# Low parts of the weights on VectorE instead of GpSimd, outside two attention loops

## The chip, the cores and the metric

The kernel runs on one core of a Trainium2 chip, alone. The metric is the time of one execution on the device in microseconds (us). In the views PE is TensorE (matrix products), DVE VectorE, ACT ScalarE, POOL GpSimd, SP the engine that issues most of the transfers. Every engine works through its own queue of instructions in order.

## What is computed

Two blocks in float32, one after the other, on a sequence of 512 tokens of width 1024, with 256 context tokens in the first. Block one has two layers, each with norm and modulation, attention (first neighborhood, then sliding window), and a squared-ReLU MLP. Block two is an even mixer (differential attention with eight heads, and an mLSTM with four) and an odd mixer (gated spatial mixing).

```python
for i in range(DEPTH):                                   # block one, two layers
    u = modulate(rms_norm(h, g_mix[i]), sh1, sc1)
    h = h + ga1 * (attention_i(u @ wqkv) @ wo)           # neighborhood, sliding window
    h = h + ga2 * squared_relu_mlp(modulate(rms_norm(h, g_mlp[i]), sh2, sc2), w1[i], w2[i])
...
p = rmsnorm(x, pre0) @ l0_w_in                           # even mixer
o_a = rmsnorm(diff_attention(q, k, v, lam)) * silu(z)
hm = rmsnorm(mlstm_chunkwise(q, k, v, i, f) * sigmoid(o)) * silu(z)
x = x + rmsnorm(concat(o_a, hm) @ l0_w_out, post0)
...
y = gelu(u) * (w_spatial * causal @ rmsnorm(gelu(v))) * silu(z)   # odd mixer, from l1_w_in
x = x + rmsnorm(y @ l1_w_out, post1)
```

## The kernel before

Activations are kept transposed: 128 channels on the partitions, tokens in the free dimension, `hl` for the 512 tokens and `hc` for the 256 of the context. A product in float32 is made of three products of parts: each operand is split into a high part, rounded to fp32r, and a low part, the remainder. `split` (L126) does it: ACT copies the source to the high part (L127), and an engine named by the caller subtracts (L128). `load_w` (L133) fetches the weights for 256 columns: two transfers on SP bring raw halves (`wraw`, four buffers), and four splits make `whi` and `wlo` (two buffers each), each a tile of 128x512. The subtractions go to `nc.gpsimd`, unless the caller names another engine. `lin` (L146) and `tok` (L155) multiply: for all chunks of the depth the high weight with both parts of the activation, and last the low weight with the high part (matmuls at L152 and L160). So `wlo` is read in the last third of a product.

The stages, by time in the profile: the first attention loop runs over eight pairs of heads `hp` (54 to 462 us); the first MLP, with the context, 560 to 1098; the sliding window loop over `t`, 1122 to 1322; the second MLP 1396 to 1728; the eight differential heads 1757 to 2030; the four mLSTM heads to 2286; the odd mixer 2365 to 2711. Between them stand `project_back` or `project_out` (products with the output weights, which are added to `hl` or `yacc` by DVE at L418 and L873) and a norm. `rstd` (L259) is the sum of a norm: ACT squares eight tiles, DVE adds them up in `acc` (L268), PE sums over the partitions (L270), ACT makes the root. The next product cannot begin before. The first MLP also carries `ada_vector` (L220), in which DVE multiplies a weight matrix by a vector (`aacc`, L229 and L231).

In a differential head (`attend` L1013) two softmax rows `p` are combined on DVE (L1037 to L1040), transposed on PE (L1043), copied to `pts` on ACT (L1045), and multiplied with the values (`PO`, L1047). Then ACT squares `PO` (L1050), DVE scales it (`t`, L1051), and makes two parts of the square (L1054, L1055) for a sum on PE (`NS`, L1056 and L1057); `gate` multiplies on POOL (L1064) and splits into `yh` and `yl`. In an mLSTM head, `finish` multiplies on POOL (L1218) and DVE (L1227) and splits into `yh` and `yl`; PE makes the states `CU` from `kw` (L1186, L1188).

The order of the instructions on each engine is set by a scheduler when the kernel is built, from the order of the code, from priorities and from estimates of how long each instruction takes. So an instruction that changes its engine moves others too.

Of the kernel before, what the change touches and what calls it, by code (L numbers as in the profile page):

```python
# [62 lines left out]
def kernel(ctx: ExitStack, tc: tile.TileContext, A, out, stop_after=None):  # L63
    nc = tc.nc
# [2 lines left out]
    wp = ctx.enter_context(tc.tile_pool(name="wp", bufs=2))  # L67
    hpool = ctx.enter_context(tc.tile_pool(name="hpool", bufs=1))
    upool = ctx.enter_context(tc.tile_pool(name="upool", bufs=1))
    scr = {}  # L70

    @contextmanager
    def scratch(name, temps, sums):
# [5 lines left out]
    def banks(**tags):  # L79

        turns.clear()
        turns.update((n, itertools.cycle(b)) for n, b in tags.items())

    def bank(n):
        b = next(turns[n])
        return psum.tile([128, 512], F32, name=n, tag=f"b{b}")
# [39 lines left out]
    def split(hi, lo, src, lo_eng):  # L126
        nc.scalar.activation(out=hi, in_=src, func=AF.Copy)  # L127
        lo_eng.tensor_tensor(out=lo, in0=src, in1=hi.bitcast(F32), op=ALU.subtract)  # L128

    def raw_w(kt, n):  # L130
        return wp.tile([128, kt, n], F32, name="wraw", tag="wraw", bufs=4)

    def load_w(parts, kt, n, lo_eng=None, room=None):  # L133
        hi, lo = room or [wp.tile([128, kt, n], F32R, name=x, tag=x) for x in ("whi", "wlo")]
        hk = kt // 2
        for s in (slice(0, hk), slice(hk, kt)):
            raw = raw_w(hk, n)
            for c0, cn, src in parts:
                nc.sync.dma_start(out=raw[:, :, c0:c0 + cn], in_=src.rearrange("(k p) f -> p k f", p=128)[:, s])
            q = hk // 2  # L140
            for x in (slice(0, q), slice(q, hk)):
                y = slice(s.start + x.start, s.start + x.stop)
                split(hi[:, y, :], lo[:, y, :], raw[:, x], lo_eng or nc.gpsimd)
        return hi, lo

    def lin(outs, w, ms, k0=0, k1=KD, start=True, stop=True):  # L146
# [217 lines left out]
    def u_lat():  # L364
        return tuple(upool.tile([128, KD, NLAT], F32R, name=x, tag=x) for x in ("uhl", "ull"))
# [17 lines left out]
    with tc.tile_pool(name="first", bufs=1) as fp, scratch("scr1", 6, 2):  # L383
# [9 lines left out]
        def u_ctx():  # L393
            return tuple(fp.tile([128, KD, NCTX], F32R, name=x, tag=x) for x in ("uhc", "ulc"))
# [133 lines left out]
        def ada_some(it, n):  # L528

            for _ in range(n):  # L530
                next(it, None)

        def neighborhood():
# [4 lines left out]
            with tc.tile_pool(name="na", bufs=1) as ap_:  # L538
# [5 lines left out]
                def qk_proj(hp, w):  # L544
                    qk = []
                    for j in range(2):
                        pl, pc = mm_tile(), mm_tile()[:, :NCTX]
                        lin([(pl, *ul), (pc, *uc)], w, slice(128 * j, 128 * j + 128))
                        g = vec("na_k") if j else nag
                        if j:  # L550
                            y = ky_tile()
                            stack_k(y, LAT, head_norm(pl, NLAT, g))
                            stack_k(y, slice(NLAT, NT), head_norm(pc, NCTX, g))
                            qk.append(y)
                        else:
                            x = qx_tile()
                            lo = next(lows)
                            stack_q((x, lo), LAT, head_norm(pl, NLAT, g))
                            nc.scalar.activation(out=x[:, :, NLAT:QC], in_=x[:, :, 0:64].bitcast(F32), func=AF.Copy)
                            nc.vector.tensor_copy(out=lo[:, :, NLAT:QC], in_=lo[:, :, 0:64].bitcast(F32))  # L560
                            stack_q((x, lo), slice(QC, QC + NCTX), head_norm(pc, NCTX, g))
                            qk.append((x, lo))
                    qks[hp] = qk

                def qk_w(hp, lo_eng=None):
                    return load_w([(0, 128, wqkv[:, 128 * hp:128 * hp + 128]),
                                   (128, 128, wqkv[:, D + 128 * hp:D + 128 * hp + 128])], KD, 256, lo_eng)

                def v_proj(g, ts=range(6)):
                    if g not in wvs:  # L570
                        wvs[g] = load_w([(0, 256, wqkv[:, 2 * D + 256 * g:2 * D + 256 * g + 256])], KD, 256)
                    if g not in vts:
                        vts[g] = vt_tile()
                    vt, wv = vts[g], wvs[g]
                    for t in ts:
                        ps = mm_tile()[:, :256]
                        x, o = (ul, 128 * t) if t < 4 else (uc, 128 * (t - 4))
                        tok(ps, wv, parts(x, slice(o, o + 128)))
                        nc.scalar.activation(out=vt[:, t, :], in_=ps, func=AF.Copy)

                def load_bias(h):
                    nc.sync.dma_start(out=biases[h % 3], in_=A["na_bias"][h])
# [80 lines left out]
                def back(o, k, c, x):  # L663
                    split(o[0][:, k, c], o[1][:, k, c], x, nc.vector)
# [12 lines left out]
                                             start=(j == 0), stop=(j == len(steps) - 1), tile_position=(0, 64 * e))  # L677

                banks(mm="01", AD="2", NS="7", S="34", PT="5", ST="6")
                for hp in range(8):  # L680
                    pv = bank("ST")
                    if hp == 7:
                        oh = (u_lat(), u_ctx())
                    for b in range(5):
                        if b == 1 and hp < 7:
                            qk_proj(hp + 1, qk_w(hp + 1))
                        if b == 1 and hp < 6:
                            v_proj(hp // 2 + 1, range(3, 6) if hp % 2 else range(3))
                        pair = [unit(hp, e, b) for e in range(2)]
                        if b == 4:  # L690
                            pc = bank("ST")
                            attend(hp, b, pair, pc)
                            if hp == 7:
                                back(oh[1], 7, slice(0, NCTX), pc[:, 0:NCTX])
                            else:
                                nc.scalar.activation(out=hc[:, hp, :], in_=pc[:, 0:NCTX], func=AF.Copy)
                        else:
                            attend(hp, b, pair, pv)
                        if b == 3:
                            for c, x in ((slice(64, NLAT), pv[:, 0:NLAT - 64]), (slice(0, 64), pv[:, NLAT - 64:NLAT])):  # L700
                                if hp == 7:
                                    back(oh[0], 7, c, x)
                                else:
                                    nc.scalar.activation(out=hl[:, hp, c], in_=x, func=AF.Copy)
                    for h in range(2 * hp + 3, min(2 * hp + 3 + 2, 16)):
                        load_bias(h)
                    if hp == 7:
                        ws = [load_w([(0, 256, A["na_wo"][:, 256 * x:256 * x + 256])], KD, 256) for x in range(1)]
                    ada_some(ada_rest, (0, 3, 3, 3, 3, 4, 4, 4)[hp])
# [17 lines left out]
        def sliding_window(u):  # L727
# [4 lines left out]
            with tc.tile_pool(name="swa", bufs=1) as ap_:  # L732
# [85 lines left out]
                    return pts, list(range(k0 // 128, k1 // 128)) + [4, 5]  # L818

                banks(mm="0", NS="7", SL="12", SC="3", PT="45", ST="6")  # L820
                for t in range(8):
                    pv = bank("ST")
                    for b in range(4):
                        if b == 1 and t < 7:
                            proj(t + 1)
                        sc = bank("SC")
                        pair = [unit(t, b, e, sc[:, 256 * e:256 * e + 256]) for e in range(2)]
                        order = pair[0][1]
                        for j, c in enumerate(order):
                            for e in (1, 0):  # L830
                                vo = 64 * (2 * (t // 4) + e)
                                nc.tensor.matmul(out=pv[64 * e:64 * e + 64, 128 * b:128 * b + 128], lhsT=vt[:, c, vo:vo + 64],
                                                 rhs=pair[e][0][:, 128 * j:128 * j + 128],
                                                 start=(j == 0), stop=(j == len(order) - 1), tile_position=(0, 64 * e))
                    split(oh[0][:, t, :], oh[1][:, t, :], pv, nc.vector)
                banks(mm="0124", NS="7")
                u = {}
                project_back(1, A["swa_wo"], (oh, None), True, norm_after(1, "mlp", u))
            return u

        stop = {None: 9, "na": 0, "mlp0": 1, "attn1": 2, "mlp1": 3, "even": 4}[stop_after]
        u = neighborhood()
        if stop >= 1:
            nu = {}
# [4 lines left out]
        if stop >= 2:  # L849
            u = sliding_window(u)  # L850
# [613 lines left out]
```

## Time and profile before

| | |
|---|---|
| median of three runs | 2733.99 us (2729.48 to 2734.04) |
| the profiled execution | 2738.25 us, its span 2736.4 us |
| busy: PE, DVE, ACT, POOL | 2603.4 (95%), 1405.6 (51%), 1254.8 (46%), 1087.3 (40%) us |
| low parts `wlo` on POOL (L128) | 628 instructions, 836.4 us |
| mean granted clock of PE | 0.99 of full speed |

The busy shares are means over stages with different limits. What a change is worth in a stage is read from the waits of the engine that sets the pace there. A wait is put down to the instruction that came last before it ended. In the timeline, instructions of one engine that follow each other at once may be shown as one row with a count.

### The profile page before, as it was taken

Reading aid. Unit: us, or ns where it says so; the run is one execution under the profiler, and the core shown is the slowest. Engines: PE = TensorE matmul, PEld = TensorE weight load, DVE = VectorE, ACT = ScalarE, POOL = GpSimd, SP = SyncE. Lnnn points to the kernel's source line nnn. Section 1 sums busy time; section 2 is a strip of 40 time slices with the busy share of each in tenths; the row PEclk is TensorE's granted clock in tenths of the full one; section 3 lists DMA queues with packets and bytes.
Section 4 is the critical chain, followed back from the end, with each engine's and each line's share of the span. In section 5 each row is a group of like instructions: output and inputs, shape, how many; then the busy total and the mean of one; then the engine's idle time right before and its main releaser. Section 6 shows DMA issues by size and latency. Waiting matters only on the chain. (4 is left out here: it accounts for less than half of the span.)

```text
span 2736.4 us, 40968 instructions
## 1 busy us (share of the span) xinstructions
PE 2603.4 (95%) x15876; PEld 2201.9 (80%) x15876; DVE 1405.6 (51%) x2908; ACT 1254.8 (46%) x2664; POOL 1087.3 (40%) x932
## 2 busy tenths in 40 slices
PE   6999998999999999899999999899999999899998
PEld 4877776788888889777888888877778888898887
DVE  4667667675666567688552222544553444502024
ACT  5655555422222223588543332466654554544342
POOL 3221313333332322533254544544435555435453
PEclk9999999999999999999999999999999999999999
DMA  7211324243333342210123333322222222322321
GB/s 246 61 55 56 107 63 153 66 135 100 114 117 118 92 124 62 74 32 19 45 88 97 93 100 100 81 62 62 67 66 78 78 83 72 97 80 91 95 87 62
DMA packets 217635, 237.94 MB, mean 87 GB/s; under 512 B 9824, under 2 KB 179296, under 8 KB 217440
## 3 DMA queue, kind: packets, MB, share of 16 engines
q1 hardware_dynamic: 210464, 229.15, 27.7%
q10 hardware_dynamic: 6976, 6.17, 0.7%
q8 instruction: 125, 2.05, 0.3%
q14 instruction: 70, 0.57, 0.1%
HBM read 233.18 MB, written 2.10 MB: 86 GB/s over the span
## 5 line engine op out<-in xcount | busy, mean ns | idle before, releaser
L128 POOL TENSOR_TENSOR wlo<-wraw,whi 128x512 fp32r<-128x512 f32 x628 | 836.4, 1361 | 887.3 <-ACT whi L127 847.3
L152 PE MATMUL mm<-uhl,whi 128*128 128x512 f32 (+1 forms) x1480 | 574.3, 391 | 3.6 <-ACT whi L127 2.6
L152 PE MATMUL mm<-ull,whi 128*128 128x512 f32 (+1 forms) x1480 | 569.9, 388 | 4.3 <-POOL ull L128 2.1
L127 ACT ACTIVATE whi<-wraw 128x512 fp32r<-128x512 f32 (+1 forms) x632 | 354.0, 619 | 445.2 <-issue 276.7
L152 PE MATMUL mm<-uhl,wlo 128*128 128x512 f32 (+1 forms) x1480 | 406.3, 386 | 0.0
L152 PEld LDWEIGHTS mm<-uhl,whi 128*128 128x128 f32 x1480 | 282.0, 191 | 62.8 <-ACT whi L127 6.1
L152 PEld LDWEIGHTS mm<-ull,whi 128*128 128x128 f32 x1480 | 282.2, 191 | 56.9 <-POOL ull L128 3.7
L152 PEld LDWEIGHTS mm<-uhl,wlo 128*128 128x128 f32 x1480 | 270.2, 190 | 54.1 <-issue 2.2
L418 DVE SCALAR_TENSOR_TENSOR hl<-mm,mod,hl 128x512 f32<-128x512 f32 (+1 forms) x156 | 105.2, 679 | 226.9 <-PE mm L152 226.9
L152 PE MATMUL mm<-h1h,whi 128*128 128x512 f32 (+1 forms) x576 | 208.4, 369 | 0.0
L152 PE MATMUL mm<-h1l,whi 128*128 128x512 f32 (+1 forms) x576 | 208.1, 369 | 0.0
L152 PE MATMUL mm<-h1h,wlo 128*128 128x512 f32 (+1 forms) x576 | 161.8, 368 | 0.0
L160 PE MATMUL mm<-whi,uhl 128*128 128x256 f32 x608 | 155.0, 290 | 1.0 <-DVE t L297 0.5
L160 PE MATMUL mm<-whi,ull 128*128 128x256 f32 x608 | 152.9, 287 | 0.0
L231 DVE SCALAR_TENSOR_TENSOR aacc<-araw,csil,aacc 128x512 f32<-128x512 f32 x196 | 148.5, 811 | 2.5 <-DMA araw<-ada_w 2.4
L304 POOL TENSOR_TENSOR t<-t,t 128x512 f32<-128x512 f32 (+1 forms) x46 | 49.1, 1067 | 231.5 <-ACT t L301 132.1
L479 DVE TENSOR_TENSOR t<-mm,t 128x512 f32<-128x512 f32 (+1 forms) x96 | 53.1, 574 | 153.2 <-ACT t L474 153.1
L474 ACT ACTIVATE t<-mm 128x512 f32<-128x512 f32 (+1 forms) x100 | 47.7, 507 | 177.8 <-PE mm L152 177.8
L152 PE MATMUL mm<-ulc,whi 128*128 128x256 f32 x448 | 124.6, 286 | 1.1 <-POOL ulc L128 1.1
L152 PE MATMUL mm<-uhc,whi 128*128 128x256 f32 x448 | 124.8, 287 | 0.0
L152 PEld LDWEIGHTS mm<-h1h,whi 128*128 128x128 f32 x576 | 108.6, 188 | 19.6 <-issue 1.0
L152 PEld LDWEIGHTS mm<-h1l,whi 128*128 128x128 f32 x576 | 108.6, 189 | 18.7
(381 smaller groups left out, 5445.2 us busy)
## 6 DMA issues: line engine op xcount, KB each, us to landing
wraw<-mlp_w SPq DMA_DIRECT2D x128, 512.0 KB, 3.8
wraw<-l_w_in SPq DMA_DIRECT2D x88, 512.0 KB, 3.7
araw<-ada_w SPq DMA_DIRECT2D x112, 256.0 KB, 3.0
wraw<-l_w_out SPq DMA_DIRECT2D x32, 512.0 KB, 3.5
wraw<-ada_w SPq DMA_DIRECT2D x24, 512.0 KB, 4.2
wraw<-l_w_in SPq DMA_DIRECT2D x48, 256.0 KB, 3.3
wraw<-na_wqkv SPq DMA_DIRECT2D x32, 256.0 KB, 3.8
wraw<-swa_wqkv SPq DMA_DIRECT2D x12, 512.0 KB, 3.6
```

The lines of the kernel that those rows point to most:

```text
L127: nc.scalar.activation(out=hi, in_=src, func=AF.Copy)
L128: lo_eng.tensor_tensor(out=lo, in0=src, in1=hi.bitcast(F32), op=ALU.subtract)
L152: nc.tensor.matmul(out=o[0], lhsT=a[:, i, ms], rhs=o[j][:, i, :], start=(start and n_ == 0), stop=(stop and n_ == len(terms) - 1))
L160: nc.tensor.matmul(out=ps, lhsT=x[:, i, :], rhs=w[:, i, :], start=(n_ == 0), stop=(n_ == len(terms) - 1))
L231: nc.vector.scalar_tensor_tensor(out=acc[v], in0=raw, scalar=x, in1=acc[v], op0=ALU.mult, op1=ALU.add)
L304: nc.gpsimd.tensor_tensor(out=q, in0=q, in1=r, op=ALU.mult)
L418: nc.vector.scalar_tensor_tensor(out=o, in0=ps, scalar=mod[i][:, 8 * which + m, v:v + 1], in1=h, op0=ALU.mult, op1=ALU.add)
L474: nc.scalar.activation(out=a, in_=p, func=AF.Relu)
L479: nc.vector.tensor_tensor(out=q, in0=p, in1=a, op=ALU.mult)
```

## The change

`scr["lo"]` holds the engine that makes the low parts in `load_w`. It is VectorE from the start; GpSimd from before the first attention loop until its last pass (`hp == 7`), and again around the sliding window loop.

```diff
-    scr = {}
+
+    scr = {"lo": nc.vector}
...
-                split(hi[:, y, :], lo[:, y, :], raw[:, x], lo_eng or nc.gpsimd)
+                split(hi[:, y, :], lo[:, y, :], raw[:, x], lo_eng or scr["lo"])
...
                 banks(mm="01", AD="2", NS="7", S="34", PT="5", ST="6")
+                scr["lo"] = nc.gpsimd
                 for hp in range(8):
                     pv = bank("ST")
                     if hp == 7:
+                        scr["lo"] = nc.vector
                         oh = (u_lat(), u_ctx())
...
                 banks(mm="0", NS="7", SL="12", SC="3", PT="45", ST="6")
+                scr["lo"] = nc.gpsimd
                 for t in range(8):
...
                     split(oh[0][:, t, :], oh[1][:, t, :], pv, nc.vector)
+                scr["lo"] = nc.vector
```

The instructions of the program are the same 588 subtractions on another engine, but the scheduler then orders all the queues anew. Three places, in the order of the queue (line numbers of the changed kernel are 1 to 5 higher).

DVE in the norm before the first MLP, before (`acc` is the sum of the squares `t`, `aacc` the running sum of `ada_vector`):

```order
783 L268 TENSOR_TENSOR acc<-acc,t_5444 128x256
784 L231 SCALAR_TENSOR_TENSOR aacc<-araw,csil,aacc 128x512
785 L268 TENSOR_TENSOR acc<-acc,t_5447 128x256
786 L231 SCALAR_TENSOR_TENSOR aacc<-araw,csil,aacc 128x512
787 L268 TENSOR_TENSOR acc<-acc,t_5450 128x256
788 L231 SCALAR_TENSOR_TENSOR aacc<-araw,csil,aacc 128x512 x3
789 L280 SCALAR_TENSOR_TENSOR t_5457<-hc,gmlp_94,rstd 128x256
```

and now:

```order
796 L269 TENSOR_TENSOR acc<-acc,t_5444 128x256
797 L232 SCALAR_TENSOR_TENSOR aacc<-araw,csil,aacc 128x512
798 L269 TENSOR_TENSOR acc<-acc,t_5447 128x256
799 L232 SCALAR_TENSOR_TENSOR aacc<-araw,csil,aacc 128x512
800 L269 TENSOR_TENSOR acc<-acc,t_5450 128x256
801 L232 SCALAR_TENSOR_TENSOR aacc<-araw,csil,aacc 128x512 x2
802 L129 TENSOR_TENSOR wlo<-wraw,whi 128x512
803 L281 SCALAR_TENSOR_TENSOR t_5457<-hc,gmlp_94,rstd 128x256
```

The rows up to the last `acc` are the same; the first `wlo` of the next weights stands behind it.

DVE in the norm at the start of the even mixer, before (`hl` is the residual stream being updated by the last product of the MLP):

```order
1862 L268 TENSOR_TENSOR acc<-acc,t_16788 128x256
1863 L268 TENSOR_TENSOR acc<-acc,t_16791 128x256
1864 L418 SCALAR_TENSOR_TENSOR hl<-mm,mod_91,hl 128x256
1865 L268 TENSOR_TENSOR acc<-acc,t_16794 128x256
1866 L268 TENSOR_TENSOR acc<-acc,t_16797 128x256
1867 L418 SCALAR_TENSOR_TENSOR hl<-mm,mod_91,hl 128x256
1868 L268 TENSOR_TENSOR acc<-acc,t_16800 128x256
1869 L268 TENSOR_TENSOR acc<-acc,t_16803 128x256
1870 L268 TENSOR_TENSOR acc<-acc,t_16806 128x256
```

and now:

```order
2013 L269 TENSOR_TENSOR acc<-acc,t_16788 128x256
2014 L129 TENSOR_TENSOR wlo<-wraw,whi 128x512
2015 L419 SCALAR_TENSOR_TENSOR hl<-mm,mod_91,hl 128x256
2016 L269 TENSOR_TENSOR acc<-acc,t_16791 128x256
2017 L129 TENSOR_TENSOR wlo<-wraw,whi 128x512
2018 L419 SCALAR_TENSOR_TENSOR hl<-mm,mod_91,hl 128x256
2019 L269 TENSOR_TENSOR acc<-acc,t_16794 128x256
2020 L129 TENSOR_TENSOR wlo<-wraw,whi 128x512
2021 L269 TENSOR_TENSOR acc<-acc,t_16797 128x256
2022 L129 TENSOR_TENSOR wlo<-wraw,whi 128x512
2023 L269 TENSOR_TENSOR acc<-acc,t_16800 128x256
2024 L129 TENSOR_TENSOR wlo<-wraw,whi 128x512
```

Between nearly every two sums a `wlo` now stands, five in front of the last one.

ACT at the end of the third differential head, before (`pts` are copies of the transposed rows, `sz` a gate, `t_17949` the square of the head's output):

```order
1302 L1045 ACTIVATE pts<-PT 128x384
1303 L997 ACT_TABLE_LOAD
1304 L997 ACTIVATE sz<-mm 128x512
1305 L1045 ACTIVATE pts<-PT 128x512
1306 L1050 ACTIVATE t_17949<-PO 128x512
1307 L127 ACTIVATE whi<-wraw 128x512 x2
```

and now:

```order
1299 L1050 ACTIVATE pts<-PT 128x384
1300 L1038 ACT_TABLE_LOAD
1301 L1038 ACTIVATE p,l_17930<-p,nm 128x512
1302 L128 ACTIVATE whi<-wraw 128x512 x4
1303 L1050 ACTIVATE pts<-PT 128x512
1304 L1002 ACT_TABLE_LOAD
1305 L1002 ACTIVATE sz<-mm 128x512
1306 L1055 ACTIVATE t_17949<-PO 128x512
```

The four `whi` of the next weights, two of which stood behind the square, now stand in front of the last `pts`.

## Rows read from the trace of the kernel before

**Rows 1.** MLP one, MLP two, odd mixer: start:end length, PE PEld DVE ACT POOL, PEclk, DMA

```profile
560.00:1098.00 538.00, 535.18 (x3306) 466.15 (x3305) 335.60 (x525) 141.28 (x290) 167.80 (x124) 1.00 0.35 106
1396.00:1728.00 332.00, 331.52 (x1567) 278.86 (x1566) 98.04 (x141) 106.27 (x197) 157.69 (x120) 1.00 0.31 96
2365.00:2711.00 346.00, 346.00 (x1941) 302.74 (x1940) 63.54 (x113) 150.43 (x302) 168.77 (x132) 1.00 0.27 83
```

**Rows 2.** waits of PE: line, what ended them; us in total, times, longest us

```profile
PE NS L270 <- DVE acc L268: 38.3, 10, 16.5
PE PT L1043 <- DVE p L1040: 8.6, 8, 2.0
PE NS L270 <- DVE pr L1007: 7.1, 1, 7.1
PE NS L1057 <- DVE t L1055: 5.1, 7, 0.7
PE CU L1188 <- DVE kw L1186: 4.9, 3, 1.7
PE mm L152 <- DVE yl L128: 2.2, 1, 2.2
```

**Rows 3.** groups by shape, wlo on POOL and on DVE: count | busy, mean ns | idle

```profile
L128 POOL TENSOR_TENSOR wlo<-wraw,whi 128x512 fp32r<-128x512 f32 x624 | 833.6, 1365 | 884.3 <-ACT whi L127 847.3 <-PE mm L152 17.3 <-issue 10.9
L128 DVE TENSOR_TENSOR wlo<-wraw,whi 128x512 fp32r<-128x512 f32 x4 | 2.6, 687 | 0.1
```

**Rows 4.** timeline, DVE and POOL, norm before the first MLP: start us, us, engine, line

```profile
526.95 1.51 DVE L268 TENSOR_TENSOR acc<-acc,t 128x256 f32<-128x256 f32 x1
528.38 1.77 DVE L231 SCALAR_TENSOR_TENSOR aacc<-araw,csil,aacc 128x512 f32<-128x512 f32 x1
533.15 0.41 DVE L268 TENSOR_TENSOR acc<-acc,t 128x256 f32<-128x256 f32 x1
533.48 0.74 DVE L231 SCALAR_TENSOR_TENSOR aacc<-araw,csil,aacc 128x512 f32<-128x512 f32 x1
526.43 6.25 POOL L128 TENSOR_TENSOR wlo<-wraw,whi 128x512 fp32r<-128x512 f32 x4 [1.41 <-ACT whi L127]
```

**Rows 5.** timeline, DVE, norm at the start of the even mixer

```profile
1735.85 2.93 DVE L268 TENSOR_TENSOR acc<-acc,t 128x256 f32<-128x256 f32 x2
1740.36 4.90 DVE L268 TENSOR_TENSOR acc<-acc,t 128x256 f32<-128x256 f32 x3
```

**Rows 6.** timeline, DVE, last head of the first attention loop

```profile
446.11 0.48 DVE L651 TENSOR_SCALAR p<-p,rl 128x512 f32<-128x512 f32 x1
447.68 1.52 DVE L651 TENSOR_SCALAR p<-p,rl 128x512 f32<-128x512 f32 x1
```

**Rows 7.** timeline, DVE and PE, norms before the second MLP and behind the even mixer

```profile
1374.68 4.32 DVE L268 TENSOR_TENSOR acc<-acc,t 128x256 f32<-128x256 f32 x5
1381.86 0.70 PE L270 MATMUL NS<-acc,ones 128*128 128x256 f32 x2 [4.23 <-DVE acc L268]
2322.08 0.96 DVE L268 TENSOR_TENSOR acc<-acc,t 128x256 f32<-128x256 f32 x1
2327.34 2.55 DVE L268 TENSOR_TENSOR acc<-acc,t 128x256 f32<-128x256 f32 x2
```

**Rows 8.** timeline, DVE and POOL, one differential head

```profile
1883.15 1.43 DVE L1039 TENSOR_SCALAR p<-p,l 128x256 f32<-128x256 f32 x1
1887.52 0.40 DVE L1039 TENSOR_SCALAR p<-p,l 128x384 f32<-128x384 f32 x1
1895.59 1.40 POOL L1064 TENSOR_TENSOR t<-t,sz 128x512 f32<-128x512 f32 x1 [11.16 <-DVE t L1051]
```

**Rows 9.** timeline, DVE, one mLSTM head

```profile
2142.89 3.35 DVE L1227 SCALAR_TENSOR_TENSOR nctionType.Sigmoid<-nctionType.Sigmoid,vecs,t 128x512 f32<-128x512 f32 x2 [0.27 <-ACT t L1225]
```

**Rows 10.** the same view as rows 1, behind the norm before the first MLP

```profile
532.70:539.50 6.80, 4.89 (x12) 3.84 (x13) 6.45 (x14) 2.98 (x7) 0.39 (x1) 0.50 0.61 194
```

**Rows 11.** timeline, ACT, another differential head

```profile
1864.30 1.15 ACT L127 ACTIVATE whi<-wraw 128x512 fp32r<-128x512 f32 x2 [1.53 <-PE mm L152]
```

## The prediction

> **What bounds the kernel now.** The stretches come first. TensorE (PE) is the bound: in the first MLP, the second MLP and the odd mixer it is busy for 535.18 of 538 us, 331.52 of 332 and 346.00 of 346 [rows 1]. Nothing that happens on VectorE (DVE) or GpSimd (POOL) can shorten those 1216 us by more than 3.3. What can be won is the time in which PE stands still, so the next view is the table of PE's waits [rows 2]. It names DVE in nearly every row that matters: the sum for the norms (acc, L268) 38.3 us in ten waits, of which one of 16.5 us lies before the first matmul and is not touched, so 21.8 remain; 7.1 us at the start of the even mixer (the name there is pr, but it stands behind the acc's, and these are late); the softmax row p in the differential heads (8.6), t L1055 there (5.1), the state kw in the mLSTM heads (4.9), yl once (2.2).
>
> Then why DVE is late there. A low part wlo takes 1365 ns on POOL and 687 ns on DVE for the same 128x512 tile [rows 3]. More important is what a running wlo does to DVE. In the norm before the first MLP an acc takes 0.41 us when POOL rests and 1.51 us beside POOL's four wlo, an aacc 0.74 and 1.77 us [rows 4]. At the start of the even mixer three acc's take 4.90 us [rows 5], where three short ones would take 1.2. In this kernel the two engines hold each other up, about 1 us a meeting.
>
> **The change, part by part.** By the order of the instructions 588 subtractions go from POOL to DVE, and 52 stay on POOL inside the two attention loops. On DVE they are 588 x 0.687 = 404 us of work. Instructions on DVE start a little before the one in front has ended: the short acc's and aacc's at 533.15, 533.48 and so on come 0.33 us apart at 0.41 us long [rows 4], so I count 0.61 us of the queue for a wlo and 0.33 for an acc. In the full stretches I cost them at nothing: in the first MLP DVE is busy for 335.60 of 538 us, a good part of that held up by POOL, in the second 98.04 of 332, in the odd mixer 63.54 of 346 [rows 1]. The cover is DVE's idle time; without it each would cost 0.61 us.
>
> Now place by place, in PE's time.
>
> A, the norm before the first MLP. Two acc's and two aacc's are each about 1.05 us too long (1.51 less 0.41, 1.77 less 0.74; one of each stands) [rows 4]. In the new order no wlo stands in front of the last acc of this norm: 4 x 1.05 = 4.2, all inside the wait with which PE starts the sum. Bounds 3 to 5.
>
> B, the last head of the first attention loop, whose loads now go to DVE too. p L651 takes 1.52 us beside POOL's wlo where another of the same shape takes 0.48 [rows 6]; nine operations of that head are too long in this way, by 7 us in all. Eleven subtractions of 0.61 us come into the same queue. I take 3; bounds 0 (they fall on the same rows) and 7 (they fall between).
>
> C, the norm before the second MLP and the one behind the even mixer's last project_out. In the first, five acc's take 4.32 us instead of about 2.0, and PE starts 7.2 us after they began, behind a wait of 4.23 [rows 7]. In the new order six acc's, one L418 (0.40) and four wlo stand there: 2.0 + 0.4 + 2.4 = 4.8, and PE follows 0.1 later: gain 2.3. In the second, from the first slow acc (0.96) to the end of the last two (2.55) it is 7.8 us [rows 7]; seven acc's, three L873 and three wlo make 2.3 + 1.0 + 1.8 = 5.1: gain 2.7, of which I take 2.4 for a slower start. Together 4.7; bounds 0 (a wlo waits for its whi in front of an acc) and 9 (no wlo is in the way).
>
> D, the norm at the start of the even mixer. From the first slow acc at 1735.85 to the end of the last at 1745.26 it is 9.4 us [rows 5]. In the new order seven acc's, two L418, five wlo, pr and one ql stand there: 2.3 + 0.8 + 3.1 + 0.1 + 0.4 = 6.7. Gain 2.7; bounds 0 and 5.4 (all the excess).
>
> E, the differential heads. In every second head POOL's four wlo meet the first softmax rows: L1039 takes 1.43 us where a larger one, unhindered, takes 0.40 [rows 8]. PE's waits for p are 8.6 us in eight, on average 1.1 [rows 2]. Three heads give 1.1 less 0.3 for the wlo that now stand between these rows, 2.4 in all; the last head, where wlo and rows alternate, 2.0. Together 4.4; bounds 0 and 8.6. The 5.1 us for t L1055 I leave as they are: what holds it up is POOL's gate product L1064, which runs there for 1.40 us [rows 8] and stays on POOL.
>
> F, the mLSTM heads. The two L1227 take 3.35 us [rows 9]; the first would take 0.61, the second still meets POOL's yl and takes 1.55: 1.2 gained in each of three heads, out of the 4.9 us for kw. In the last head POOL has three wlo queued in front of a product that yl needs, and the 2.2 us for yl go [rows 2]. Together 5.8; bounds 2 and 7.
>
> G, the clock. After a long wait PE runs for a while at the lower of its two levels, 1.2 GHz: a granted clock of 0.50 for 6.8 us after the wait of A, with 4.89 us of matmuls in it [rows 10], which would take half at 2.4 GHz: 2.45. A stretch after yl's wait costs 1.7. These two I count as gone, 4.2; the others stay, since most of a wait stays in front of them. Bounds 0 and 10.
>
> H, new waits. In heads 0, 2 and 4 of the differential attention ScalarE (ACT) now has four whi in front of the last pts, and whi waits until PE has released the weight buffer. Two such whi take 1.15 us behind a wait of 1.53 [rows 11], so four are 2.3 and pts follows 0.6 later: 2.9. Between the release and the product that reads pts PE has eleven matmuls of 128x512, at 331.52/1567 = 0.21 us [rows 1] 2.3 us. That leaves 0.6, with the hand-overs about 1 in each of three heads: 3; bounds 0 and 7 (the whole 2.3 three times).
>
> The sum is 4.2 + 3 + 4.7 + 2.7 + 4.4 + 5.8 + 4.2 - 3 = 26.0 us. The profiled execution took 2738.25 us, 4.3 above the median of the runs shown, 2733.99. So 2738.25 - 26.0 - 4.3 gives 2708.0: **2708**. Late next at A, C and D is DVE still, then ACT's squares.
>
> **Rivals.** *The meetings stay.* Some 290 operations remain on POOL outside the loops (ull, yl, gates, t L304), and each of the 588 is now one that they can meet. If half of what A to F win comes back in this form, 24.8 become 12.4, the clock gives 1 and H costs 3: 10.4, or 2723.6. For it speaks that t L1055 meets POOL's gate in all eight heads [rows 8]; against it that POOL's work falls by 588 x 1.365 = 800 us. The Trainium skill, page "SBUF — State Buffer", section "Who interferes with whom", says that a VectorE instruction with two SBUF inputs contends with a GpSimd instruction that reads SBUF, and that whoever issues first keeps the other out for the whole instruction. The rows agree (1.51 us against 0.41); and by this rule a moved subtraction, with its two inputs, is itself such an instruction.
>
> *The exchange is even.* At C, D and E the wlo stand in front of the last acc or between the rows, and take from the same chain what the meetings took. If they arrive late or take 0.9 us of the queue, C and D keep 4 of 7.4, B and E nothing, the clock nothing, A and F their 10, and H costs 10: 4 in all, 2730.
>
> *Slower: DVE stands behind its own wlo.* Of POOL's idle time 847.3 us were waits of a wlo for its whi [rows 3]; that cost nothing, since hardly anything else was queued there. On DVE the evictions L418 and L479, the acc's and the softmax rows are queued behind each wlo. PE runs on while free PSUM banks last, up to seven of twelve or more matmuls, 7 x 12 x 0.21 = 18 us; a wait of DVE that is longer stops it. If one in two of the 143 moved loads stopped PE for 1 us, 72 less 26 leave 46 us: 2780. Against it: in the new order nearly every wlo stands behind the work that is due before it.
>
> **Chances.** Forecast 0.73, the meetings stay 0.11, the even exchange 0.09, slower 0.07. The range runs from 2690, where B to H go 18 of the 25 us to their better bounds, to 2729, which takes in the second case and half of the third. A measurement of this kernel can tell about 0.2%, 5.5 us, from no change. Faster by more: the first case and most of the second, 0.82; within it 0.11; slower 0.07.
>
> **What would show it.** DVE's work up by 404 us less what the meetings took (1 us each), POOL's down by 800; acc at 0.41 us in the norm before the first MLP, and PE's wait there near 1 us; PE's waits for acc, without the first, near 13 us; L1039 below 0.5 us in the heads; two fewer stretches at 1.2 GHz; the full stretches within 1 us of what they were. It is wrong if PE waits for evictions or for wlo inside the MLPs, if acc keeps its two lengths in the norms, or if ACT's whi in front of pts stop PE for more than 2 us a head.

## The result and the profile after

The changed kernel takes 2671.83 us (median of five runs, 2669.24 to 2673.70) where the kernel before takes 2732.59; the ratio is 0.9779 with an interval of 0.9765 to 0.9793. That is 60.8 us faster, where 26.0 were forecast, with a range that ended at 2690. The direction and the mechanism on VectorE were right, the size was not: what the new order does to PE's own queue was left out, and most of the clock with it.

The profiled execution has a span of 2667.5 us, 68.9 less than that of before. PE's busy time fell by 21.8 us, from 2603.4, and its idle time by 47.1. Some 8 of the 68.9 us are which executions were profiled: that of before took 5.7 us more than its median, that of now 2.6 less. The shares of the engines, then what is left of PE's waits (as in [rows 2]), then the full stretches (as in [rows 1]):

```profile
PE 2581.6 (97%) x15876; PEld 2185.8 (82%) x15876; DVE 1611.9 (60%) x3496; ACT 1249.7 (47%) x2661; POOL 314.9 (12%) x344
```

```profile
PE NS L271 <- DVE acc L269: 22.3, 10, 14.8
...
PE NS L1062 <- DVE t L1060: 5.1, 7, 0.7
...
PE mm L153 <- POOL ull L129: 2.9, 5, 1.0
...
PE mm L153 <- DVE wlo L129: 1.9, 3, 0.8
```

```profile
541.10:1076.40 535.30, 534.81 (x3306) 466.27 (x3305) 361.77 (x652) 142.40 (x293) 6.39 (x8) 1.00 0.35 109
1364.80:1696.40 331.60, 331.60 (x1567) 278.94 (x1566) 163.27 (x263) 107.46 (x200) 0.00 (x0) 1.00 0.31 96
...
2296.10:2642.10 346.00, 346.00 (x1941) 302.74 (x1940) 121.57 (x225) 150.48 (x302) 25.60 (x20) 1.00 0.27 83
```

The waits for acc, without the first one, are 7.5 us instead of 21.8, and those for pr, p, kw and yl are gone. DVE's busy time rose by 206 us although 404 us of work came to it. Of the difference, some 150 us are meetings that no longer happen: added up one by one in the trace, the lengths of DVE's other instructions fell from 1542 to 1391 us. The rest is mostly that instructions which follow each other at once overlap by 0.08 us, so a subtraction adds less than its length. The groups by shape show the same (line, form, count, busy us, mean ns; acc before and after):

```profile
L129 DVE TENSOR_TENSOR wlo<-wraw,whi 128x512 fp32r<-128x512 f32 x576 | 384.2, 706 | 380.8 <-ACT whi L128 248.3 <-PE mm L153 81.0 <-PE mm L161 50.4
...
L268 DVE TENSOR_TENSOR acc<-acc,t 128x256 f32<-128x256 f32 x101 | 64.5, 638 | 22.6 <-ACT t L266 19.3
...
L269 DVE TENSOR_TENSOR acc<-acc,t 128x256 f32<-128x256 f32 x101 | 43.6, 432 | 13.6 <-ACT t L267 11.4
...
L1232 DVE SCALAR_TENSOR_TENSOR nctionType.Sigmoid<-nctionType.Sigmoid,vecs,t 128x512 f32<-128x512 f32 x8 | 5.6, 747 | 0.0
```

Where the time went, stage by stage, from the two profiled executions. A stage ends in both where PE has issued the same number of matmuls; the clock's column is the length of the stretches at 1.2 GHz.

| stage (us in the trace of before) | length before, after | PE idle before, after | at 1.2 GHz before, after |
|---|---|---|---|
| the start (to 54) | 54.3, 51.7 | 22.1, 19.0 | 0, 0 |
| first loop, without its last head (54 to 410) | 355.8, 352.7 | 17.7, 16.3 | 3.4, 0 |
| its last head (to 462) | 52.1, 47.6 | 7.4, 5.5 | 3.4, 0 |
| norms before the first MLP (526 to 560) | 34.1, 25.1 | 8.4, 2.6 | 10.2, 0 |
| first MLP (to 1098) | 537.8, 535.3 | 2.8, 0.5 | 0, 0 |
| norms before the sliding window (to 1122) | 24.0, 18.1 | 5.7, 1.6 | 3.4, 0 |
| norm before the second MLP, with its product (1322 to 1396) | 74.0, 69.4 | 5.9, 2.7 | 3.4, 0 |
| start of the even mixer (1728 to 1757) | 29.0, 20.7 | 7.3, 1.2 | 10.2, 0 |
| differential heads (to 2030) | 273.1, 260.0 | 19.3, 10.6 | 3.4, 0 |
| mLSTM heads (to 2286) | 256.0, 251.3 | 5.0, 0.7 | 0, 0 |
| behind the even mixer (to 2365) | 78.9, 67.7 | 10.5, 4.6 | 13.7, 0 |

The other stages differ by less than 1.1 us. In this execution not one of the eleven stretches at 1.2 GHz inside the program is left, only the one at its end. The four other executions of the changed kernel have a mean granted clock of 0.996 or 0.997; one stretch of 3.4 us takes 0.0006 off the mean, so by this estimate they have one to four such stretches inside. The mean granted clock (the line of the core, before and after):

```profile
core 0: 2736.4 us, clock 0.989
```

```profile
core 0: 2667.5 us, clock 0.998
```

And the norm at the start of the even mixer, which had the longest wait inside the program [rows 2, 5], in the timeline (PE before; then DVE and PE after):

```profile
1745.31 1.22 PE L270 MATMUL NS<-acc,ones 128*128 128x256 f32 x2 [7.09 <-DVE pr L1007]
```

```profile
1707.37 0.41 DVE L269 TENSOR_TENSOR acc<-acc,t 128x256 f32<-128x256 f32 x1
1707.70 0.68 DVE L129 TENSOR_TENSOR wlo<-wraw,whi 128x512 fp32r<-128x512 f32 x1
1708.31 0.41 DVE L269 TENSOR_TENSOR acc<-acc,t 128x256 f32<-128x256 f32 x1
...
1707.50 0.50 PE L153 MATMUL mm<-uhl,wlo 128*128 128x256 f32 x2 [0.83 <-DVE wlo L129]
...
1710.90 0.70 PE L271 MATMUL NS<-acc,ones 128*128 128x256 f32 x2 [0.17 <-DVE acc L269]
```

The sums take 0.41 us each and the wlo between them 0.68, as the prediction counted. But PE, which had stood still for 7.09 us in front of this sum, is now nearly always busy with products that use the new wlo; it waits 0.83 us for one of these and 0.17 us for the sum. In front of this sum PE has 41 matmuls of the next product in its queue; before it had 16. The scheduler filled up in the same way at three more norms: 26 instead of 16 before the second MLP, 32 instead of 19 at the context norm, and 12 more behind the even mixer. In the norm before the first MLP nothing changed there.

### The profile page after: what moved, and what is told of

The parts are those of the page before. It is cut to its first block, busy times and chain, and to the rows that moved or that the text cites. A ratio compares the mean times of both kernels' runs of the same rounds, so it can differ in the third digit from the quotient of the medians.

```text
span 2667.5 us, 40938 instructions
## 1 busy us (share of the span) xinstructions
PE 2581.6 (97%) x15876; PEld 2185.8 (82%) x15876; DVE 1611.9 (60%) x3496; ACT 1249.7 (47%) x2661; POOL 314.9 (12%) x344
## 4 chain that ended last, share of the span: by engine, by line
PE 80%; DVE 10%; ACT 7%; issue 2%; DMA 1%; POOL 0%; DVEq 0%; POOLq 0%; ACTq 0%; SPq 0%
PE mm L153 59%; PE mm L161 7%; PE ST L677 1%; DVE t L281 1%; PE PT L656 1%; PE ST L836 1%; PE PT L819 1%; PE NS L300 1%; DVE acc L269 1%; PE S L347 1%; PE PO L1052 1%; ACT qx L327 1%; DVE wlo L129 1%; ACT whi L128 1%; ACT qx L333 1%
## 5 line engine op out<-in xcount | busy, mean ns | idle before, releaser
L129 DVE TENSOR_TENSOR wlo<-wraw,whi 128x512 fp32r<-128x512 f32 (+1 forms) x580 | 385.7, 704 | 383.6 <-ACT whi L128 248.3
L129 POOL TENSOR_TENSOR ull<-t,uhl 128x256 fp32r<-128x256 f32 (+1 forms) x40 | 37.7, 947 | 1091.5 <-ACT uhl L128 997.8
L232 DVE SCALAR_TENSOR_TENSOR aacc<-araw,csil,aacc 128x512 f32<-128x512 f32 x196 | 135.2, 746 | 0.0
L161 PEld LDWEIGHTS mm<-whi,uhl 128*128 128x128 f32 x608 | 116.2, 191 | 2.7 <-DVE t L298 1.4
## 6 DMA issues: line engine op xcount, KB each, us to landing
araw<-ada_w SPq DMA_DIRECT2D x112, 256.0 KB, 2.9
wraw<-l_w_in SPq DMA_DIRECT2D x48, 256.0 KB, 3.4
wraw<-na_wqkv SPq DMA_DIRECT2D x32, 256.0 KB, 4.0
```

Of the source, the lines that this page charges most:

```text
L161: nc.tensor.matmul(out=ps, lhsT=x[:, i, :], rhs=w[:, i, :], start=(n_ == 0), stop=(n_ == len(terms) - 1))
L232: nc.vector.scalar_tensor_tensor(out=acc[v], in0=raw, scalar=x, in1=acc[v], op0=ALU.mult, op1=ALU.add)
```

## Theories

*Meetings:* the gain is that DVE and POOL no longer hold each other up; whether it is the wlo that runs on POOL does not matter, only that POOL reads SBUF. *Readiness:* the gain is that a wlo is done sooner, and that the scheduler therefore puts more of the next product in front of the sums. *The clock* amplifies either. The experiments are the changed kernel with one thing put back or moved on, unless something else is said.

## Experiments

**e1 and e2: work on GpSimd that nobody reads.** The order of the other engines is left as it is.

```diff
+        if n == 256:
+            nc.gpsimd.tensor_copy(out=dmy[:, 0:1], in_=hs(2)[:, 0:1])
+            for _ in range(4):                                                # e1
+                nc.gpsimd.tensor_tensor(out=dmy, in0=dmy, in1=dmy, op=ALU.mult)
+            for _ in range(10):                                               # e2
+                nc.gpsimd.memset(dmy, 0.0)
```

> The changed kernel (2671.8 us) plus work on GpSimd that nobody reads: in each norm over 256 columns, once the third tile of its input is there, one copy of a column and four products 128x512 of two SBUF operands (about 5.5 us a norm). The order on TensorE, VectorE and ScalarE is the same as in the changed kernel, instruction by instruction. If the gain came from the meetings of VectorE and GpSimd, acc takes 1 us or more again in these norms, TensorE's waits for acc come back at eight or nine norms with 2 to 4 us each, and so do stretches at 1.2 GHz: 2692 to 2707 us. If it came from wlo being ready sooner, or from the new order alone: 2671 to 2676 us.

> As e1, with ten memsets of 128x512 in place of the four products, about as long in all (5.5 us a norm) and at the same places; again the order on the other engines is that of the changed kernel. If a GpSimd instruction holds VectorE up because it reads SBUF, a memset does not: acc stays at 0.41 to 0.47 us, 2671 to 2677 us. If any busy GpSimd does it, or what counts is the ull and other work queued behind on GpSimd, the time is that of e1: 2692 to 2707 us.

e1 takes 2695.21 us, 23.4 more than the changed kernel, e2 2673.33, 1.5 more. The same wlo, the same place in DVE's queue, beside products (e1; DVE, POOL) and beside memsets (e2; DVE, POOL):

```profile
1716.08 1.52 DVE L131 TENSOR_TENSOR wlo<-wraw,whi 128x512 fp32r<-128x512 f32 x1
...
1715.95 3.72 POOL L270 TENSOR_TENSOR dmy<-dmy 128x512 f32<-128x512 f32 x3
```

```profile
1705.00 0.68 DVE L131 TENSOR_TENSOR wlo<-wraw,whi 128x512 fp32r<-128x512 f32 x1
...
1706.00 0.41 DVE L275 TENSOR_TENSOR acc<-acc,t 128x256 f32<-128x256 f32 x1
...
1704.53 1.70 POOL L270 MEMSET dmy<- 128x512 f32 x3
```

PE's waits for acc, in e1 and in e2:

```profile
PE NS L277 <- DVE acc L275: 36.9, 11, 17.9
```

```profile
PE NS L277 <- DVE acc L275: 23.5, 9, 14.8
```

Beside products this wlo takes 1.52 us, beside memsets 0.68, and the next acc there 0.41. So what holds DVE up is not that POOL is busy, nor what is queued there, but what it does. The Trainium skill, page "SBUF — State Buffer", section "Who interferes with whom", says that a VectorE instruction with two SBUF inputs contends with a GpSimd instruction that reads SBUF, not with one that only writes it; the two runs agree. e1 also shows the prediction's first rival at work on the moved subtractions themselves. Of the 25.5 us between the profiled executions of e1 and of the changed kernel, 10.6 lie behind the even mixer, where PE's idle time rose by 7.7.

**e3, e9 and e12: the filling in front of the sums.** PE's matmuls beyond a given number are queued behind the sum, as they were before. e3 does it at the start of the even mixer, e9 and e12 at four norms. A few instructions on DVE and ACT change places with them: at the start of the even mixer six wlo instead of five stand in front of the last acc.

```diff
-                nc.tensor.matmul(out=o[0], lhsT=a[:, i, ms], rhs=o[j][:, i, :], ...)
+                with tc.issue_after(hold.ins) if hold and n_ >= free else nullcontext():
+                    nc.tensor.matmul(out=o[0], lhsT=a[:, i, ms], rhs=o[j][:, i, :], ...)
...
-                qk_proj(0, w0, HALF[x:x + 1])
-                v_proj(0, range(2 * x, 2 * x + 2))
+                qk_proj(0, w0, HALF[x:x + 1], None if x else half_sum)
+                with nullcontext() if x else tc.issue_after(half_sum.ins):
+                    v_proj(0, range(2 * x, 2 * x + 2))
```

> The changed kernel with one thing put back as it was before, at the start of the even mixer alone: on TensorE only the first 16 matmuls of the next projection may stand in front of the norm's sum, the 25 others of it stand behind (as in the kernel before). If the gain at this norm (8.3 us) is largely the longer filling in front of the sum, TensorE waits there 3 to 4 us again (25 x 0.12), with a stretch at 1.2 GHz behind it: 3 to 7 us slower, 2675 to 2679. If the gain is that of the shorter chain on VectorE alone: no change, 2671 to 2673.

> As e3, but at four norms: the start of the even mixer, the norm before the second MLP, the context norm before the sliding window and the norm behind the even mixer's last project_out. In front of each sum TensorE has again as many matmuls of the next product as in the kernel before (16, 16, 19 and 12, where the changed kernel has 41, 26, 32 and 24). If the longer filling is what the prediction missed, e3's 5.8 us grow by 1 to 2 us of waiting at each of the three others, with a stretch at 1.2 GHz behind some: 2680 to 2690 us. If it counts at the even mixer alone: 2677 to 2679.

> e9 mended at its fourth place. There e9 held back three products too many behind the sum; now exactly the twelve matmuls stand behind it that stood behind it in the kernel before, and the four norms have the filling of before. The three other places gave back 9 us in e9. If the filling is what the prediction missed there too: 12 matmuls, 1.4 us of waiting and a longer one at 1.2 GHz, 2 to 5 us on top of the nine: 2682 to 2686 us. If the filling does not count at the fourth place: 2680 to 2682.

e3 takes 2677.61 us, 5.8 more; e9 2688.17, 16.3 more; e12 2682.12, 10.3 more. In e9 the fourth place held three products too many back, and PE waited 10.3 us there, nearly twice as long as in the kernel before; so of e9 only the other three places count, and e12 is the one to read. At the context norm e12 (like e9) still goes too far: 15 matmuls stand in front of the sum where the kernel before has 19, which at 0.12 us each is about 0.5 us of its wait there. In e12, PE's waits for acc, the wait at the start of the even mixer, and the clock around its end:

```profile
PE NS L272 <- DVE acc L270: 32.8, 9, 15.0
```

```profile
1716.18 1.22 PE L272 MATMUL NS<-acc,ones 128*128 128x256 f32 x2 [5.36 <-DVE acc L270]
```

```profile
1713.30:1720.20 6.90, 4.02 (x15) 3.60 (x16) 4.60 (x11) 1.54 (x5) 0.00 (x0) 0.51 0.86 227
```

The wait of 7.09 us falls to 5.36 with the filling of before, so by the faster DVE, and from there to 0.17 by the filling. At the three other norms (before the second MLP, context, behind the even mixer) the waits were 4.23, 2.73 and 5.36 us before, are 2.71, 2.35 and 3.40 in e12, and 0.53, 0.32 and 1.98 in the changed kernel:

```profile
1353.07 0.70 PE L271 MATMUL NS<-acc,ones 128*128 128x256 f32 x2 [0.53 <-DVE acc L269]
...
2266.61 0.67 PE L271 MATMUL NS<-acc,ones 128*128 128x256 f32 x2 [1.98 <-DVE acc L269]
```

So at these four norms more than half of what PE won is the order of its own queue, which is worth about 10 of the 60.8 us, the clock included. Why the scheduler filled up so was not taken apart.

**e4: the gate product on VectorE.**

```diff
-                nc.gpsimd.tensor_tensor(out=t, in0=t, in1=szs[h // 2][h % 2], op=ALU.mult)
+                nc.vector.tensor_tensor(out=t, in0=t, in1=szs[h // 2][h % 2], op=ALU.mult)
```

> The changed kernel with the gate product of the eight differential heads (t times sz) on VectorE instead of GpSimd. If it is GpSimd's product that holds up the low part of the square, that operation takes 0.69 instead of 1.66 us, TensorE's seven waits for it (5.1 us in the changed kernel too) fall below 1 us in all: 3 to 5 us faster, 2667 to 2669. If the product stands in the same chain on VectorE instead: within 1 us of 2671.8.

2665.58 us, 6.3 less, a little more than the 3 to 5 expected. The low part of the square (line 1060 in this kernel too; min, median, max in ns) took 1658 ns in the changed kernel (the median), and now:

```profile
L1060 DVE TENSOR_TENSOR t<-t,t x8: 679/683/685, 1763.9 to 1966.3; 128x512 fp32r<-128x512 f32 x8
```

PE's idle time in the stage fell by 4.0 us. What the prediction said of this wait, that POOL's gate product makes it and keeps it, was right.

**e5 and e13: the differential heads.** Low parts of the loads back on GpSimd, in e5 inside the loop over the heads, in e13 up to the end of the product behind it.

```diff
             banks(mm="012", NS="7", S="34", PT="5", PO="6")
+            scr["lo"] = nc.gpsimd
             for h in range(8):
...
+            scr["lo"] = nc.vector            # e5
             gate_rows(ps)
             project_out(A["l0_w_out"][0:D, :], (yh, yl), yacc, True)
+            scr["lo"] = nc.vector            # e13
```

> The changed kernel with the low parts of the loads inside the loop over the eight differential heads back on GpSimd. This stage is 13.1 us shorter in the changed kernel than before. If it is the low parts of this stage that did it, the 13 us come back: 2682 to 2686 us, with TensorE's waits for the softmax rows at 8 us again. By the prediction's own terms for this stage (4.4 us, with one stretch at 1.2 GHz 6): 2676 to 2678.

> e5, with the loads of the product behind the differential heads (project_out) on GpSimd as well. e5 gave back 7.8 us of the 13.1 of this stage. If the rest is the last head, where the low parts of these loads meet the softmax rows: the stage is back at 271 to 273 us, 2683 to 2686 us in all. If it is the new order of the stage that no low part on GpSimd brings back: 2679 to 2681.

e5 takes 2678.87 us, 7.0 more, which lies between its two expected ranges, with 7.8 of the stage's 13.1 back; e13 2683.29, 11.5 more, with 12.6 back. PE's waits for the softmax rows in e5 and e13:

```profile
PE PT L1048 <- DVE p L1045: 5.7, 6, 1.5
```

```profile
PE PT L1048 <- DVE p L1045: 8.6, 8, 2.0
```

8.6 us is what they were before [rows 2]. So nearly all of this stage is the low parts, and some 5 us of it those of the output weights, which meet the last head's rows. Both runs put back the meetings together with POOL's slower subtraction and the order that goes with it; how much each is worth was not taken apart.

**e6: the full stretches.**

```diff
-                        w = load_w([(0, 256, w1[...])], KD, 256)
+                        w = load_w([(0, 256, w1[...])], KD, 256, nc.gpsimd if g > 1 else None)
...
-                        ws.append(load_w([(0, 512, w2[...])], 4, 512))
+                        ws.append(load_w([(0, 512, w2[...])], 4, 512, nc.gpsimd if g < 6 else None))
...
-                w = load_w([(0, 256, wi[...])], KD, 256)
+                w = load_w([(0, 256, wi[...])], KD, 256, nc.gpsimd)
```

> The changed kernel with the low parts back on GpSimd inside the stretches that TensorE fills: the loads of both MLPs but for their first and last ones, and the input loads of the odd mixer, some 270 of the 588 moved subtractions. If nothing on VectorE or GpSimd counts while TensorE is full: 2670 to 2674 us, with VectorE held up about 1 us a meeting again and nobody waiting. If the change also paid there: 3 to 8 us slower.

2674.43 us, 2.6 more, a little above the expected range. In the profiled executions the three stretches are as long as in the changed kernel (535.0, 331.6 and 346.1 us), and most of the difference lies in four single stretches at 1.2 GHz in stages that the edit does not touch; such stretches of 3.4 us (1.7 us of time each) come and go from run to run. So 256 of the 588 moved subtractions are worth 2.6 us at most, and in the three stretches themselves nothing, as forecast.

**e7, e8, e10 and e11: further on.** e7 has no low part of a weight on GpSimd at all; e8 has the changed kernel's loads, with ull, ulc, the odd halves of the residual sum, and the gate and yl of the differential heads on VectorE; e10 is both; e11 moves the rest of the arithmetic as well.

```diff
-                scr["lo"] = nc.gpsimd                                   # e7, e10, e11: at both loops
+                scr["lo"] = nc.vector
...
-                split(uh, ul, t, nc.gpsimd)                             # e8, e10, e11
+                split(uh, ul, t, nc.vector)
...
-            (nc.gpsimd if k % 2 else nc.vector).tensor_tensor(out=hl[:, k, c], ...)
+            nc.vector.tensor_tensor(out=hl[:, k, c], ...)
...
-        nc.gpsimd.tensor_tensor(out=q, in0=q, in1=r, op=ALU.mult)       # e11, and others like it
+        nc.vector.tensor_tensor(out=q, in0=q, in1=r, op=ALU.mult)
```

> The changed kernel with VectorE also inside the two attention loops of the first block, so that no low part of a weight is made on GpSimd at all (52 more subtractions, 36 us of work on VectorE). In these loops VectorE is busy for 280 of 408 us and 156 of 200. If the meetings cost more than the subtractions even there: 2 to 6 us faster, 2666 to 2670. If VectorE sets the pace in the loops: 2 to 10 us slower, 2674 to 2682.

> The changed kernel with nearly all that still meets VectorE in norms and heads moved off GpSimd: the low parts ull and ulc of the modulated input, yl and the gate of the differential heads, and the odd halves of the residual sum behind the mixers. If meetings are what is left to win, TensorE's waits for ull and ulc (4.7 us) and for the square (5.1) go: 5 to 10 us faster, 2662 to 2667. If these operations now stand in VectorE's chain in front of what TensorE waits for: no gain or up to 6 us slower, 2672 to 2678.

> e7 and e8 in one: no low part of a weight on GpSimd anywhere, and the work of norms and differential heads on VectorE. The two gains (10.3 and 26.9 us) lie in different stages; if they add up: 2633 to 2637 us. If VectorE becomes the bound in the loops: 2640 to 2650.

> e10, and the rest of the arithmetic off GpSimd too (the products in head_norm, rope, finish and the odd mixer), so that GpSimd is left with copies, casts and memsets. If what meetings are left still cost: 2 to 10 us faster than e10. If these products now lengthen VectorE's chains in the attention loops, where it is busy for some 70% of the time: up to 10 us slower than e10.

e7 takes 2661.50 us (10.3 less, where at most 6 were expected), e8 2644.97 (26.9 less, where 5 to 10 were), e10 2635.87 and e11 2632.95, which is 0.963 of the kernel before (0.9617 to 0.9643) and the best of all. The gains of e7 and e8 nearly add up in e10 (36.0 of 37.2). e8 moves only 84 instructions, and wins nearly half of what the 588 won: its instructions stand in the norms and heads, where PE waits. PE's waits for acc in e8, and the engines in e11:

```profile
PE NS L271 <- DVE acc L269: 17.0, 3, 15.0
```

```profile
PE 2569.0 (98%) x15876; PEld 2189.7 (83%) x15876; DVE 1658.6 (63%) x3732; ACT 1257.2 (48%) x2667; POOL 41.3 (2%) x108
```

Even in the attention loops, where DVE is the busiest, the move pays: e7 shortens the two loops by 8.4 and 2.3 us. How much of e8's gain is the meetings and how much the faster engine on PE's path was not taken apart.

Put back one at a time, the filling at four norms (10.3 us), the differential heads (11.5) and the full stretches (2.6) account for 24 of the 60.8 us; what the other places are worth is read from the two traces alone.

## Why the prediction was wrong in size, step by step

The terms for VectorE's chain at the norms were about right. Two terms came out beyond their own bounds: D (measured 6.9, upper bound 5.4) and G, the clock (21.8, upper bound 10). E, F and H came out at their better bounds (8.7, 7.1 and nothing lost).

*What bounds the kernel, and the full stretches:* right; each changed by at most 2.5 us together with what stands at its ends, and e6 shows that next to nothing in them counts.

*A, forecast 4.2:* the wait of 5.15 us became 0.97, which is 4.2. Here the queue of PE did not change, and the count of too-long operations was the whole story of the wait (before, after):

```profile
534.61 1.22 PE L270 MATMUL NS<-acc,ones 128*128 128x256 f32 x2 [5.15 <-DVE acc L268]
...
520.26 0.70 PE L271 MATMUL NS<-acc,ones 128*128 128x256 f32 x2 [0.97 <-DVE acc L269]
```

*B, 3:* 1.9 us of idle time in the last head, and a stretch at 1.2 GHz.

*C, 4.7, and D, 2.7:* measured 7.1 (4.23 to 0.53, and 5.36 to 1.98) and 6.9 (7.09 to 0.17). With the filling of before, in e12, it is 3.5 and 1.7. So the terms as counted, on DVE's chain, were somewhat too high (5.2 where 7.4 were counted), and the part that was not counted, PE's filling, was larger than they (8.8). The step that failed was to read the new order on DVE and ACT at these norms and not on PE: there the rows between the last product and the sum would have told that 41 matmuls now stood where 16 had stood. The context norm, left out of the sum, won 2.4 us too, most of it in this way. The rival of an even exchange (the wlo in front of the last acc take what the meetings took) was half right for DVE, where C and D keep 5.2 of their 7.4 us in e12 and the rival has 4; it fell for the same reason: PE has work meanwhile.

*E, 4.4:* the waits for p fell from 8.6 us to none, and the stage's idle time by 8.7. The subtraction of the wlo between the rows was wrong: no wait of PE for p is left.

*F, 5.8:* the waits for kw and yl, 7.1 us, are gone. The second L1227 did not meet POOL's yl as assumed; the operation takes 747 ns on average where [rows 9] show 3.35 us for two.

*G, the clock, 4.2:* this is the term that was mis-sized most. In the profiled execution all eleven stretches went, not two, and PE's busy time fell by 21.8 us; the eleven held 43.2 us of matmuls, and half of that is 21.6. I had kept the others "since most of a wait stays in front of them"; with the filling no such wait was left, the longest being 2.0 us. The stretches at the four norms hold 17.8 us of those matmuls, so 8.9 of the 21.8; the others stand elsewhere. e12 shows the link: with waits of 5.36, 3.40 and 2.35 us back, so are stretches of 6.8, 3.4 and 3.4 us at their ends. It is not a strict one: a wait of 2.71 us in e12 has no stretch, three more stretches there stand where no wait just before was above 2.0 us, and e2, e4 and e6 have two to four where the changed kernel's profile has none. So part of G is which execution was profiled.

*H, -3:* nothing of it. PE has no wait for the last pts; the four whi in front of it ran back to back and found their buffer released.

Forecast 26.0, measured 68.9 in the profiled executions and 60.8 by the medians. By the medians 35 were missed, by the profiled executions 43. Of the 43, 17.6 are the clock, and the rest is idle time: 6.6 at C and D, 4.3 at E, 3 at H, 2.4 at the context norm, 1.3 at F, 3.1 at the start, and smaller pieces in the first loop and the first MLP. The start had been held untouched, but the first wait for acc is 14.8 us where it was 16.5, and with the products of e1 17.9. The first rival, that meetings with what is left on GpSimd persist, was true as a mechanism: e4 and e8 show 6.3 and 26.9 us still to be won. How much it took from the gain of this change no run shows; the moved subtractions take 706 ns on average where four on DVE took 687.

## What to carry to other kernels

Look at the engine that waits before anything else: when an operation gets faster, the scheduler may put other work into the wait, and a gain that is counted on the chain alone is then too small. In this kernel two-input work on GpSimd was paid for twice, by its own slowness (1365 against 687 ns) and by what it does to VectorE; work that only writes cost 1.5 us for ten memsets a norm. Where PE's waits fall to 2 us or less, count the clock as well: it gave a third of the 68.9 us here.

## What the runs showed of the hardware

GpSimd products of two SBUF operands stretched a VectorE subtraction of 128x512 from 0.68 to 1.52 us, memsets in the same place left it at 0.68 (e1, e2). The two programs differ by 21.9 us, with the same order on every other engine. The stretches at 1.2 GHz cost the kernel before 21.8 us in all, though its mean granted clock reads 0.989; a mean so near to 1 hides them.

A meeting can outlast one instruction of GpSimd. At the start of the even mixer in the kernel before, one acc (DVE) was held through three subtractions that followed each other on POOL:

```profile
1740.87 3.85 DVE L268 TENSOR_TENSOR acc<-acc,t 128x256 f32<-128x256 f32 x1
...
1740.74 3.70 POOL L128 TENSOR_TENSOR wlo<-wraw,whi 128x512 fp32r<-128x512 f32 x3
```

It is the only one of its kind in that trace, where every other instruction of DVE is at most 1.25 us longer than the shortest of its group, and it makes 3.4 of the 9.4 us in which the prediction saw meetings of "about 1 us" at D.
